# A cast on ScalarE in place of a second comparison on VectorE, while the first and third coefficient tables are built

## The chip, the cores and the metric

The kernel runs on one core of one Trainium2 chip. The metric is the device time of one execution in microseconds (us); lower is better. The engines are named as in the profile: PE (TensorE matmuls), PEld (its weight loads), DVE (VectorE), ACT (ScalarE), POOL (GpSimd) and SP (SyncE, which here only issues DMAs).

## The reference, cut to what matters

One transformer layer runs over 640 tokens of 1024 numbers: 128 context tokens and 512 latent tokens, that is five blocks of 128 tokens. The change lies in the second half of the layer, a retrieval from 16,384 single-neuron experts:

```
s1, s2 = scores of the query halves against 128 keys each, per head (8 heads)
v1, i1 = top_k(s1, 16);  v2, i2 = top_k(s2, 16)
top, sel = top_k(v1[:, None] + v2[None, :], 16)      # 16 experts a head
eidx = i1 * 128 + i2 of the chosen ones;  gate = softmax(top)
act = gelu(x . u[eidx])                               # one dot product per chosen expert
y = sum over 8 heads x 16 of gate * act * v[eidx]
```

Each token thus has 128 chosen experts (8 x 16), each with a coefficient `gate * act`, and each expert number splits into a first key `eidx >> 7` and a second key `eidx & 127`.

## The kernel before

**The u side.** For all five blocks the rows `u[eidx]` are gathered: one indirect DMA of POOL per chosen expert fetches one row of 1024 numbers for each of the 128 tokens (512 KB), and one DVE instruction (`scalar_tensor_tensor` over 1024 columns) makes the 128 dot products. There are 640 such gathers, in order of the blocks, 128 a block. The text calls the pair of them "a gather".

**The v side.** For block 4 the rows of v are gathered in the same way (128 more gathers at the very end). For blocks 0 to 3 they are not: there the sum over experts is a dense product with all of v, on PE. For it each block needs a **table** of 128 x 128 coefficients per token, most of them zero. `Dense.build(b)` makes the table of block b (b = 0, 1, 2, 3: the first to the fourth table), and `Dense.product(g)` multiplies two tables with v, which is streamed in by SP as 128 pieces of 512 KB: product 0 takes the first and second table, product 1 the third and fourth.

**One table.** The inner loop of `build` runs 64 times, over two tokens each; the text calls one turn **a pair**. For the two tokens, with the 128 chosen experts on the partitions, it makes two one-hot matrices of 128 x 128: `B_` from the second keys and `A_` from the first keys, the latter scaled by the coefficients. Two matmuls (`B_` transposed times `A_`, 128 x 128 x 128) then give the tables of the two tokens. The engines share a pair as follows: DVE compares a row of numbers 0 to 127 (`iota2`, bf16) with the keys twice, once into `eq` (bf16, 256 columns) and once into `B_` (f32, 256 columns); ACT multiplies `eq` by the coefficients into `A_` (two instructions of 128 columns); PE does the two matmuls; and after every second pair ACT copies 512 columns from PSUM into the table, strided for the first two tables and dense for the other two. `eq` and the pair `A_`, `B_` have two buffers each, used in turn. Table b = 2q' + q lies in memory `W[q]`, so the third table overwrites the first one while product 0 still reads it: rows n to n+3 of it are written once product 0 has used them.

**Order.** `Plan` records every instruction, gives each an estimated cost, and lists them by a forward and backward pass over the engines; each engine then runs its list strictly in order. A changed instruction therefore moves others too: which gathers, top-k steps and matmuls stand between the pairs is decided anew. Main work (lane 0) and gathers (lane 1) compete for DVE. All instructions are issued from one line, L365, so the profile is read by operation and tile. In it `arena` is the large SBUF tile in which tables, one-hot matrices and streamed rows lie, `iota` is `iota2`, `w` are the buffers of streamed weights and of v, `dots` the dot products.

**Stages.** The key scores of blocks 2 to 4 (`key_scores`, matmuls 128 x 384 with weights wq) run on PE while the first table is begun; then the rest of the first table and the second; then product 0, with the third table beside its second half and the beginning of the fourth at its end; then the rest of the fourth; then product 1, beside the last u gathers and all v gathers.

Of the kernel before, what the change touches and what calls it, by code (L numbers as in the profile page):

```python
# [12 lines left out]
BF16 = mybir.dt.bfloat16  # L13
# [3 lines left out]
AF = mybir.ActivationFunctionType  # L17
OP = mybir.AluOpType
# [3 lines left out]
P = 128  # L22
# [346 lines left out]
def layer(ctx: ExitStack, tc: tile.TileContext, a: dict):  # L369
    nc = Plan(tc.nc)  # L370
# [9 lines left out]
    iota2 = st.tile([P, P, 2], BF16, name="iota2")  # L380
# [32 lines left out]
    def bank():  # L413
        return ps.alloc([512], lo=banks[0], hi=banks[1])
# [11 lines left out]
    def mm(out, lhsT, rhs, start, stop):  # L426
        nc.tensor.matmul(out, lhsT=lhsT, rhs=rhs, start=start, stop=stop)
        k, m = lhsT.shape[0], int(np.prod(lhsT.shape[1:]))
        n = int(np.prod(rhs.shape[1:]))
        up = lambda v: 32 if v <= 32 else 64 if v <= 64 else 128  # L430
        clk["PE"] += 4 * n / 2400.0 * up(k) / 128 * up(m) / 128

    def tr(out, in_):
        nc.tensor.transpose(out, in_, ident)
        clk["PE"] += 0.216
# [118 lines left out]
    oneh, eqs, tabs, scb, spare = [], [], [], [], []  # L554

    def reserve():

        all_ = ar.alloc([19, P], lo=0, hi=12 * 256 // UNIT).ap
        oneh[:] = [all_[:, 4 * i:4 * i + 4].rearrange("s (z n) i -> s z n i", z=2) for i in range(2)]
        eqs[:] = [all_[:, 8 + i].bitcast(BF16).rearrange("s (i n) -> s i n", n=2) for i in range(2)]  # L560
        tabs[:] = [all_[:, 12], all_[:, 13], all_[:, 14].bitcast(BF16).rearrange("s (z n) -> s z n", z=2)]
        scb[:] = [all_[:, 15:19]]
        spare[:] = [all_[:, 0:8].rearrange("s a b -> s (a b)")]
# [388 lines left out]
    def ctx_front():  # L952
# [123 lines left out]
        ada(2, 1)  # L1076
        make_gates(0, ("g2",))
        reserve()
        done.add("ctx")

# [471 lines left out]
    class Dense:  # L1552
# [5 lines left out]
        def build(self, b):  # L1558

            g, q = divmod(b, 2)  # L1560
            if self.W[q] is None:
                self.W[q] = ar.alloc([P, P], top=True)
            Wn = self.W[q].ap
            if g == 0:
                Wn = Wn.rearrange("j i n -> j n i")
            while (b, 3) not in cready:
                yield "wait"

            bt = bank()
            tr(bt.ap[:, 0:P], cw[b].rearrange("q h k -> q (h k)"))  # L1570
            cT, ti, keys = tabs
            tii = ti.bitcast(I32)
            id_ = idx[b].rearrange("q h k -> q (h k)")
            for z, (op, s) in enumerate(((OP.arith_shift_right, 7), (OP.bitwise_and, 127))):
                nc.vector.tensor_single_scalar(tii, id_, s, op=op)
                nc.vector.tensor_scalar(ti, tii, 1.0, None, op0=OP.mult)
                tr(bt.ap[:, P * (z + 1):P * (z + 2)], ti)
            nc.scalar.copy(cT, bt.ap[:, 0:P])
            nc.scalar.copy(keys, bt.ap[:, P:3 * P].rearrange("s (z n) -> s z n", z=2))
            ps.free(bt)  # L1580
            full = None
            for m in range(P // 2):
                n0 = 2 * m
                while g == 1 and self.at < min(n0 + 4, P) and n0 % 4 == 0:
                    yield "at"
                eq, A_, B_ = eqs[m % 2], oneh[m % 2][:, 0], oneh[m % 2][:, 1]
                nc.vector.tensor_tensor(eq, iota2, keys[:, 0, None, n0:n0 + 2].to_broadcast([P, P, 2]), op=OP.is_equal)
                nc.vector.tensor_tensor(B_, iota2.rearrange("s i n -> s n i"),
                                        keys[:, 1, n0:n0 + 2, None].to_broadcast([P, 2, P]), op=OP.is_equal)
                if n0 % 4 == 0:  # L1590
                    bw = bank()
                for k in range(2):
                    nc.scalar.activation(A_[:, k], eq[:, :, k], AF.Copy, scale=cT[:, n0 + k:n0 + k + 1])
                if full is not None:
                    nc.scalar.copy(*full)
                    ps.free(last)
                    full = None
                for k in range(2):
                    z = n0 % 4 + k
                    mm(bw.ap[:, P * z:P * z + P], B_[:, k], A_[:, k], True, True)  # L1600
                if n0 % 4:
                    full, last = (Wn[:, n0 - 2:n0 + 2, :], bw.ap.rearrange("j (n i) -> j n i", n=4)), bw
                    yield
            nc.scalar.copy(*full)
            ps.free(last)
# [194 lines left out]
```

## Time and profile before

| what | value |
|---|---|
| time, median of 3 runs | 1915.19 us (1913.91 to 1916.84) |
| the profiled execution's own time | 1923.32 us |
| its span | 1921.6 us |
| DMA moved in the span | 651.92 MB, 339 GB/s in the mean |
| PE, DVE, ACT busy in the span | 94%, 77%, 28% |

The profiled execution took 8.1 us (0.4%) longer than the median of the runs. Its span covers the program on the engines; 1.7 us lie around it. Busy shares are means over stages of very different kinds, so the stages are read one by one. A busy PE is not PE at its peak, since matmuls overlap.

### The profile page before, as it was taken

The page shows a single profiled execution, that of the slowest core. Times are in us where ns is not written, and L with a number is a line of the kernel's source. Part 1 is how long each engine was busy: PE and PEld are TensorE (multiplying, and loading weights), DVE is VectorE, ACT ScalarE, POOL GpSimd, SP SyncE. Part 2 cuts the span into 40 slices and gives each one's busy share as a digit, 9 for nine tenths or more (in the row PEclk, how much of TensorE's full clock was granted, in tenths as well). Part 3 has the DMA queues.
Part 4 walks back from the last instruction along what each step waited for, and adds up shares of the span by engine and source line. Part 5 has one row for each costly group of instructions (what it writes and reads, how often), then busy time and mean ns, then how long its engine had stood idle before and what let it go on. Part 6 is the DMA issues. An engine that isn't in the chain of part 4 may idle for free.

```text
span 1921.6 us, 21158 instructions
## 1 busy us (share of the span) xinstructions
PE 1801.0 (94%) x6096; PEld 1088.0 (57%) x6096; DVE 1471.6 (77%) x3785; ACT 534.2 (28%) x1368; POOL 823.9 (43%) x779
## 2 busy tenths in 40 slices
PE   7989999989899979978999999899987999999997
PEld 2437454445866556666544444455565666666665
DVE  2246897875788899999999998777999565666666
ACT  1125320223434333788311120122565000000000
POOL 0000456660034456433646544444434444444442
PEclk9998999988989989855999999899997999999999
DMA  9896878985668899866999999999988999999998
GB/s 363 311 328 246 305 246 311 386 327 177 209 232 305 311 342 396 307 207 179 337 408 408 399 397 410 378 408 407 388 256 276 410 409 409 409 410 409 409 409 335
DMA packets 200428, 651.92 MB, mean 339 GB/s; under 512 B 22380, under 2 KB 25708, under 8 KB 200184
## 3 DMA queue, kind: packets, MB, share of 16 engines
q0 software_dynamic: 110592, 402.70, 56.1%
q1 hardware_dynamic: 89720, 247.87, 34.5%
q8 instruction: 49, 0.80, 0.2%
q14 instruction: 67, 0.55, 0.1%
HBM read 639.22 MB, written 11.27 MB: 339 GB/s over the span
## 4 chain that ended last, share of the span: by engine, by line
DMA 28%; PE 27%; DVE 15%; issue 4%; ACT 2%; POOL 0%; DVEq 0%; SPq 0%; POOLq 0%; ACTq 0%
PE psum L365 27%; DMA arena<-in_u,idx 13%; DMA arena<-in_v,idx 12%; DVE arena L365 10%; ACT arena L365 2%; DVE psum L365 1%; DVE i L365 1%; DVE oh L365 1%; DMA out_y<-w 1%; DVE vi L365 1%; DMA w<-xres 1%; POOL arena L365 0%; DVE cand L365 0%; DMA arena<-in_w_out 0%; DVE idx L365 0%
## 5 line engine op out<-in xcount | busy, mean ns | idle before, releaser
L365 PE MATMUL psum<-w,arena 128*128 128x512 f32 (+1 forms) x2580 | 1105.1, 600 | 12.2 <-DVE arena L365 6.5
L365 POOL DMA_INDIRECT arena<-in_u,idx x640 | 701.1, 1096 | 929.5 <-DVE arena L365 466.4
L365 PEld LDWEIGHTS psum<-w,arena 128*128 128x128 f32 (+1 forms) x2580 | 567.2, 228 | 458.9 <-issue 296.2
L365 PE MATMUL psum<-arena 128*128 128x128 f32 (+5 forms) x2436 | 543.0, 381 | 62.7 <-DVE arena L365 35.8
L365 PEld LDWEIGHTS psum<-arena 128*128 128x128 f32 (+2 forms) x2436 | 380.3, 219 | 265.3 <-issue 144.9
L365 DVE SCALAR_TENSOR_TENSOR arena<-arena 128x1024 f32<-128x1024 f32 (+6 forms) x451 | 488.2, 1092 | 39.7 <-DMA arena<-in_u,idx 35.4
L365 DVE SCALAR_TENSOR_TENSOR arena<-arena,psum 128x1024 f32<-128x1024 f32 x256 | 308.2, 1214 | 82.3 <-DMA arena<-in_u,idx 82.3
L365 ACT ACTIVATE arena<-arena 128x128 f32<-128x128 bf16 (+8 forms) x626 | 240.0, 432 | 270.3 <-PE psum L365 119.8
L365 ACT COPY arena<-psum 128x512 f32<-128x512 f32 (+3 forms) x360 | 203.9, 579 | 316.9 <-PE psum L365 287.6
L365 DVE SCALAR_TENSOR_TENSOR psum<-arena,cw,psum 128x1024 f32<-128x1024 f32 x127 | 163.6, 1288 | 94.7 <-DMA arena<-in_v,idx 94.5
L365 DVE TENSOR_TENSOR arena<-iota,arena 128x256 f32<-128x256 bf16 (+1 forms) x512 | 162.9, 356 | 39.8 <-PE psum L365 35.0
L365 POOL DMA_INDIRECT arena<-in_v,idx x128 | 119.9, 936 | 144.3 <-DVE psum L365 115.6
L365 PE MATMUL psum<-arena,w 128*128 128x128 f32 (+1 forms) x704 | 142.0, 362 | 1.4 <-ACT arena L365 1.4
L365 PEld LDWEIGHTS psum<-arena,w 128*128 128x128 f32 x704 | 103.0, 200 | 32.5 <-ACT arena L365 2.1
L365 PE MATMUL psum<-ident,arena 128*128 128x128 f32 x372 | 66.5, 313 | 31.6 <-DVE arena L365 28.4
L365 PEld LDWEIGHTS psum<-ident,arena 128*128 128x128 f32 x372 | 51.0, 163 | 62.6 <-DVE arena L365 36.0
L365 DVE TENSOR_TENSOR arena<-arena 128x256 f32<-128x256 f32 (+7 forms) x131 | 59.8, 497 | 6.7 <-ACT arena L365 4.3
L365 DVE TENSOR_TENSOR arena<-psum,arena 128x512 f32<-128x512 f32 (+1 forms) x40 | 27.3, 687 | 40.8 <-PE psum L365 40.2
L365 ACT ACTIVATE zz<-dots 128x64 f32<-128x64 f32 x10 | 2.6, 256 | 186.9 <-DVE arena L365 186.9
L365 DVE TENSOR_REDUCE arena<-arena 128x8 f32<-128x512 f32 (+1 forms) x17 | 12.7, 745 | 42.1 <-ACT arena L365 42.1
L365 ACT ACTIVATE vi<-i 128x32 f32<-128x32 uint32 x20 | 4.7, 235 | 137.7 <-DVE i L365 137.6
L365 DVE MAX8 vi<-arena 128x8 f32<-128x128 f32 x128 | 31.1, 280 | 14.4 <-ACT arena L365 14.4
(75 smaller groups left out, 529.9 us busy)
## 6 DMA issues: line engine op xcount, KB each, us to landing
w<-in_v SPq DMA_DIRECT2D x251, 512.0 KB, 6.8
w<-in_wq SPq DMA_DIRECT2D x44, 512.0 KB, 4.8
w<-in_w_ada SPq DMA_DIRECT2D x41, 512.0 KB, 6.1
w<-in_w_in SPq DMA_DIRECT2D x24, 512.0 KB, 7.8
w<-in_w_out SPq DMA_DIRECT2D x20, 512.0 KB, 6.1
arena<-in_u,idx POOLq DMA_INDIRECT x640, 7.5
arena<-in_w_in SPq DMA_DIRECT2D x16, 512.0 KB, 10.5
arena<-in_x SPq DMA_DIRECT2D x9, 512.0 KB, 6.4
```

The lines of the kernel that those rows point to most:

```text
L365: getattr(getattr(self.nc, eng), fn)(*args, **kw)
```

## The change

`eq` becomes twice as wide (its second half lies in memory that was reserved and not used). In `build(0)` and `build(2)` (q = 0) one comparison of 512 columns in bf16 makes both one-hot matrices at once, the first keys' in `eq[:, 0]` and the second keys' in `eq[:, 1]`, and ACT casts the latter into `B_` (256 columns, bf16 to f32). In `build(1)` and `build(3)` nothing changes but the address of `eq`.

```diff
-        eqs[:] = [all_[:, 8 + i].bitcast(BF16).rearrange("s (i n) -> s i n", n=2) for i in range(2)]
+        eqs[:] = [all_[:, 8 + 2 * i:10 + 2 * i].rearrange("s a b -> s (a b)").bitcast(BF16)
+                  .rearrange("s (z i n) -> s z i n", z=2, n=2) for i in range(2)]
...
                 eq, A_, B_ = eqs[m % 2], oneh[m % 2][:, 0], oneh[m % 2][:, 1]
-                nc.vector.tensor_tensor(eq, iota2, keys[:, 0, None, n0:n0 + 2].to_broadcast([P, P, 2]), op=OP.is_equal)
-                nc.vector.tensor_tensor(B_, iota2.rearrange("s i n -> s n i"),
-                                        keys[:, 1, n0:n0 + 2, None].to_broadcast([P, 2, P]), op=OP.is_equal)
+                if q:
+                    nc.vector.tensor_tensor(eq[:, 0], iota2, keys[:, 0, None, n0:n0 + 2].to_broadcast([P, P, 2]),
+                                            op=OP.is_equal)
+                    nc.vector.tensor_tensor(B_, iota2.rearrange("s i n -> s n i"),
+                                            keys[:, 1, n0:n0 + 2, None].to_broadcast([P, 2, P]), op=OP.is_equal)
+                else:
+                    nc.vector.tensor_tensor(eq, iota2[:, None].to_broadcast([P, 2, P, 2]),
+                                            keys[:, :, None, n0:n0 + 2].to_broadcast([P, 2, P, 2]), op=OP.is_equal)
+                    nc.scalar.copy(B_, eq[:, 1].rearrange("s i n -> s n i"))
                 if n0 % 4 == 0:
                     bw = bank()
                 for k in range(2):
-                    nc.scalar.activation(A_[:, k], eq[:, :, k], AF.Copy, scale=cT[:, n0 + k:n0 + k + 1])
+                    nc.scalar.activation(A_[:, k], eq[:, 0, :, k], AF.Copy, scale=cT[:, n0 + k:n0 + k + 1])
```

Counted over the program, DVE loses 256 comparisons of 256 columns and gains 128 of 512; ACT gains 128 casts of 256 columns; PE, POOL and the DMAs keep their numbers. What the new order does is shown at three places.

**PE, where the key scores end.** The 128x384 rows are the last matmuls of the key scores, the 128x128 rows between them those of the first table (two a pair; of the long row 12 are the last scores), the `ident` rows transposes that prepare the second table. Before:

```order
L365 MATMUL psum<-arena,w_92 128x384
L365 MATMUL psum<-arena 128x128 x2
L365 MATMUL psum<-arena,w_92 128x384 x2
L365 MATMUL psum<-arena 128x128 x2
L365 MATMUL psum<-arena,w_92 128x384 x2
L365 MATMUL psum<-arena 128x128 x70
L365 MATMUL psum<-ident,cw_73 128x128
L365 MATMUL psum<-ident,arena 128x128
```

With the change:

```order
L365 MATMUL psum<-arena,w_91 128x384 x8
L365 MATMUL psum<-arena,w_92 128x384 x6
L365 MATMUL psum<-arena 128x128 x2
L365 MATMUL psum<-arena,w_92 128x384 x2
L365 MATMUL psum<-arena 128x128 x92
L365 MATMUL psum<-ident,cw_73 128x128
L365 MATMUL psum<-ident,arena 128x128
```

Before, 24 of the first table's 64 pairs stand among the key scores on PE and 40 behind them; with the change 19 stand among them and 45 behind.

**ACT, in the part of the first table behind the key scores.** ACTIVATE 128x128 makes half of an `A_`, CAST 128x256 is the new cast, COPY 128x4x128 the strided copy of two pairs into the table. With the change:

```order
L365 CAST arena<-arena 128x256
L365 ACTIVATE arena<-arena 128x128 x2
L365 COPY arena<-psum 128x4x128
L365 ACTIVATE arena<-arena 128x128
L365 CAST arena<-arena 128x256
L365 ACTIVATE arena<-arena 128x128
L365 CAST arena<-arena 128x256
L365 ACTIVATE arena<-arena 128x128 x2
L365 COPY arena<-psum 128x4x128
```

Before, the same pairs read:

```order
L365 ACTIVATE arena<-arena 128x128 x2
L365 COPY arena<-psum 128x4x128 x2
L365 ACTIVATE arena<-arena 128x128 x4
L365 COPY arena<-psum 128x4x128
L365 ACTIVATE arena<-arena 128x128 x4
L365 COPY arena<-psum 128x4x128
```

Each pair's two ACTIVATEs are joined by one CAST; the strided copies stay.

**DVE, at the end of the fourth table.** SCALAR_TENSOR_TENSOR 128x1024 is a gather's dot product, TENSOR_TENSOR `arena<-iota` a comparison (two a pair). Before, the last rows of the table are:

```order
L365 TENSOR_TENSOR arena<-iota_65,arena 128x256 x3
L365 SCALAR_TENSOR_TENSOR arena,dots_77<-arena,psum 128x1024
L365 TENSOR_TENSOR arena<-iota_65,arena 128x256 x4
L365 SCALAR_TENSOR_TENSOR arena,dots_77<-arena,psum 128x1024
L365 TENSOR_TENSOR arena<-iota_65,arena 128x256
L365 SCALAR_TENSOR_TENSOR arena,dots_77<-arena,psum 128x1024
L365 TENSOR_TENSOR arena<-iota_65,arena 128x256 x3
L365 SCALAR_TENSOR_TENSOR arena,dots_77<-arena,psum 128x1024
L365 TENSOR_TENSOR arena<-iota_65,arena 128x256
L365 SCALAR_TENSOR_TENSOR arena,dots_77<-arena,psum 128x1024
L365 TENSOR_TENSOR arena<-iota_65,arena 128x256 x3
```

With the change:

```order
L365 TENSOR_TENSOR arena<-iota_65,arena 128x256 x2
L365 TENSOR_TENSOR w_90<-w_90 128x256
L365 SCALAR_TENSOR_TENSOR arena,dots_77<-arena,psum 128x1024
L365 TENSOR_TENSOR arena<-iota_65,arena 128x256 x4
L365 SCALAR_TENSOR_TENSOR arena,dots_77<-arena,psum 128x1024
L365 TENSOR_TENSOR arena<-iota_65,arena 128x256 x3
L365 SCALAR_TENSOR_TENSOR arena,dots_77<-arena,psum 128x1024
L365 TENSOR_TENSOR arena<-iota_65,arena 128x256 x4
L365 SCALAR_TENSOR_TENSOR arena,dots_77<-arena,psum 128x1024
L365 TENSOR_TENSOR arena<-iota_65,arena 128x256 x3
L365 SCALAR_TENSOR_TENSOR arena,dots_77<-arena,psum 128x1024
L365 TENSOR_TENSOR arena<-iota_65,arena 128x256 x4
```

Five gathers stand here among 15 comparisons before and among 20 with the change. Among the fourth table's last 32 pairs there are 19 gathers before and 14 with the change, and four more of the small instructions that finish blocks 0 and 1 (as the `w_90` row). On PE, the table matmuls behind the last mixed rows and ahead of product 1's long run (cut there only by one or two single matmuls of product 1) belong to 41 pairs before and to 37 with the change; 502 product matmuls are left at that point in both.

## Rows read from the trace of the kernel before

**Rows 1.** The chain that ended last, in order of time: start, us, what.

```profile
689.46 104.77 PE psum L365 x435
...
1217.72 198.73 PE psum L365 x694
...
1488.25 14.73 DMA arena<-in_u,idx
```

**Rows 2.** Busy time by stretch (start:end, length, engines, PE clock, DMA share, GB/s).

```profile
core 0: us, PE busy (x) PEld busy (x) DVE busy (x) ACT busy (x) POOL busy (x), PEclk, DMA share, GB/s
705.50:801.80 96.30, 94.94 (x434) 65.67 (x433) 93.86 (x268) 51.61 (x121) 58.85 (x50) 1.00 1.00 380
801.80:842.30 40.50, 30.75 (x129) 27.49 (x130) 36.11 (x115) 34.65 (x83) 13.74 (x14) 0.55 0.66 201
842.30:883.50 41.20, 35.29 (x131) 28.80 (x130) 40.45 (x124) 35.33 (x87) 15.13 (x16) 0.54 0.71 215
883.50:925.00 41.50, 34.54 (x135) 28.00 (x134) 39.56 (x101) 35.37 (x83) 16.23 (x15) 0.57 0.60 179
945.00:1209.00 264.00, 262.74 (x615) 116.22 (x614) 241.21 (x842) 34.82 (x102) 137.37 (x120) 1.00 1.02 405
1218.00:1388.00 170.00, 170.00 (x576) 90.60 (x576) 138.62 (x310) 59.13 (x167) 81.34 (x87) 0.99 1.01 395
1425.00:1479.00 54.00, 35.83 (x169) 29.96 (x167) 50.14 (x129) 35.89 (x99) 21.15 (x22) 0.74 0.79 248
1488.00:1872.00 384.00, 384.00 (x896) 264.41 (x895) 234.57 (x272) 2.42 (x8) 173.23 (x185) 1.00 1.03 409
```

**Rows 3.** DVE's timeline: start, us, what; a last bracket is idle time before.

```profile
787.47 0.69 DVE L365 TENSOR_TENSOR arena<-iota,arena 128x256 bf16<-128x256 bf16 x2
...
801.08 1.16 DVE L365 TENSOR_TENSOR arena<-iota,arena 128x256 f32<-128x256 bf16 x4
...
817.55 0.28 DVE L365 TENSOR_TENSOR arena<-iota,arena 128x256 bf16<-128x256 bf16 x1
817.75 0.08 DVE L365 MATCH_VALUE_LOAD w<-vi,w 128x8 f32 x1
...
842.01 0.41 DVE L365 TENSOR_TENSOR arena<-iota,arena 128x256 f32<-128x256 bf16 x1
...
842.87 1.21 DVE L365 SCALAR_TENSOR_TENSOR arena<-arena 128x1024 f32<-128x1024 f32 x1
...
844.00 0.42 DVE L365 TENSOR_TENSOR arena<-iota,arena 128x256 f32<-128x256 bf16 x1
844.34 0.27 DVE L365 TENSOR_TENSOR cand<-vi 128x64 f32<-128x64 f32 x1
```

**Rows 4.** Groups by engine, operation and shape: busy us, mean ns of one.

```profile
L365 ACT ACTIVATE arena<-arena 128x128 f32<-128x128 bf16 x512 | 172.3, 394 | 146.9 <-PE psum L365 114.6 <-DVE arena L365 30.0 <-DVE vi L365 0.3
...
L365 ACT ACTIVATE arena<-arena 128x512 f32<-128x512 f32 x25 | 15.4, 627 | 20.8 <-DVE arena L365 20.5
...
L365 ACT ACTIVATE zz<-dots 128x64 f32<-128x64 f32 x10 | 2.6, 256 | 186.9 <-DVE arena L365 186.9
```

**Rows 5.** ACT's timeline in the first table.

```profile
815.38 1.04 ACT L365 COPY arena<-psum 128x512 f32<-128x512 f32 x1 [0.38 <-PE psum L365]
816.21 1.27 ACT L365 ACTIVATE arena<-arena 128x128 f32<-128x128 bf16 x4
...
822.92 1.91 ACT L365 COPY arena<-psum 128x512 f32<-128x512 f32 x2
...
843.14 0.39 ACT L365 ACTIVATE arena<-arena 128x128 f32<-128x128 bf16 x1
```

**Rows 6.** PE's timeline, at the third table's preparation and at product 1's start.

```profile
1217.72 0.48 PE L365 MATMUL psum<-ident,arena 128*128 128x128 f32 x1 [7.87 <-DVE arena L365]
...
1226.39 7.03 PE L365 MATMUL psum<-w,arena 128*128 128x512 f32 x16
...
1479.16 11.14 PE L365 MATMUL psum<-w,arena 128*128 128x512 f32 x22 [0.68 <-ACT arena L365]
```

**Rows 7.** The page's first line.

```profile
span 1921.6 us, 21158 instructions
```

## The prediction

> **What bounds the kernel now.** I read the chain of waits first, then busy time by stretch, then the timelines. The chain [rows 1] runs over PE where the key scores end (689.5 to 794.2 us) and from 1217.7 on while product 0 and the third table run together; behind 1488 it runs over gathers in flight. The stretches [rows 2] tell how hard that is. In 945 to 1209 (product 0) PE is busy 262.74 of 264 us and the DMAs are full (share 1.02, 405 GB/s). In 1218 to 1388 PE is busy throughout, and in 1488 to 1872 both PE (384 of 384) and the DMAs (409 GB/s) are. There no saving on DVE or ACT can shorten anything. Three stretches have slack on both: the first table behind the key scores (801.8 to 842.3, PE clock 0.55, so about the 1.2 GHz level, DMA share 0.66), the second table (842.3 to 925, likewise), and the rest of the fourth (1425 to 1479, DMA share 0.79). In all three DVE is busiest: 36.11 of 40.5, then 40.45 of 41.2 and 39.56 of 41.5, then 50.14 of 54 us. ACT has 34.65 of 40.5 in the first. So the end moves by what these three stretches gain or lose, since all behind product 1's start is full.
>
> **Price of a pair.** On DVE what counts is the distance of starts. A bf16 comparison of 256 columns starts 0.20 us ahead of the next instruction, an f32 one 0.34 [rows 3]. If the first runs at two columns in the time the second takes for one, 256 columns cost 0.14 fast and 0.28 slow, and the fixed part is 0.06. The new comparison of 512 columns, all bf16, then takes 0.06 + 0.28 = 0.34, and a pair falls from 0.54 to 0.34: 0.20 saved, 128 times, 25.6 us of DVE. Slow it would be 0.62, that is 0.08 more than before. The operands have the same kind of pattern as those of the 256-column one, so I take 0.34.
>
> No cast from SBUF of 256 columns is in the trace. ACT takes 256 ns for 64 columns and 627 ns for 512 [rows 4]; on the line between, 256 columns take 415 ns. The starts of successive ACTIVATEs lie (1.27 - 0.394) / 3 = 0.29 apart [rows 4, 5], 0.10 less than the 394 ns one lasts, so a cast holds ACT for 0.32 us. Bounds: 0.29, as one of 128 columns, and 0.43, half of a strided copy of 512, whose starts lie 1.91 - 1.04 = 0.87 apart [rows 5]. Over 128 pairs that is 41 us of new ACT work for 25.6 of DVE.
>
> The Trainium skill, "ScalarE: Activation LUTs", Rules for kernel authors, says that simple elementwise work belongs on VectorE, which per element is up to about three times as fast in bf16; that speaks against this change. Here the instruction that leaves DVE writes f32 and holds it for 0.34 us, no less than the cast holds ACT, so the trace shows no such advantage for it. The same page's figures (186 ns + 0.833 ns a column, 93 ns overlap) make the cast 0.31 as an estimate; 42 casts (below) would then sum to 0.4 us less.
>
> **First table.** Up to pair 22 PE works off key scores, and DVE is full (93.86 of 96.3 us to 801.8). Counted in the order, DVE has made 50 gathers by pair 22 instead of 45 since the table's start. A gather holds it for 844.00 - 842.87 = 1.13 us [rows 3]. So +5.7 for gathers, -22 x 0.20 = -4.4 for comparisons, about +1 for small instructions that moved ahead: pair 22, which now leaves DVE at 787.5 [rows 3], leaves it at about 790, and ACT starts on it then. From there to pair 64 ACT has 42 x (2 x 0.29 + 0.32) = 37.8 us for pairs, 18 strided copies x 0.87 = 15.7, and some 2.5 of small work (one wide cast of the top-k, the gelu): 56 us. DVE has less: over the last 32 pairs 16 gathers x 1.13 + 32 x 0.34 + some 8 of small work = 37, as long as before; there ACT has 44. So ACT becomes the bound and pair 64 leaves it no earlier than 846, with 3 to 4 us of waiting for PE and DVE at about 849.5. Now it leaves ACT at 843.1 [rows 5]. **+6.4 us**; without any wait +3, with as much idle time as ACT has now (5.9 us in 40.5) up to +10.
>
> **Second table.** Unchanged on ACT (35.3 us a half [rows 2]) and DVE-bound. The order gives DVE 33 gathers instead of 34 and 7 small instructions instead of 22 between pairs 64 and 128, since they went ahead while ACT was the bound: -1.1 and -15 x 0.2 (they start 0.2 to 0.3 apart) = -4. **-3.5**, bounds -1 and -5.
>
> **Product 0 and third table.** PE waits 7.87 us for the third table's preparation, which DVE reaches behind its gathers [rows 6]. In both orders 132 gathers lie between pair 128 and that instruction, and the DMAs that bring them are full, so the wait moves along unchanged; 12 small instructions fewer are worth 0 to -2: I take -1. The third table's 64 casts (20 us of ACT) lie beside PE's full 170 us, where ACT is busy 59.13; the 13 us that DVE saves there lie under the same cover. Were ACT late by its whole 20 us there, product 0 would end as much later.
>
> **Fourth table.** With the change 37 pairs instead of 41 are left when PE has nothing else. PE does the other 4 x 2 matmuls of 128 columns under cover but pays for them: a 512-column one takes 7.03 / 8 = 0.88 [rows 6], so 8 x 0.22 = +1.8. DVE, 50.14 of 54 us busy, has four pairs less (4 x 0.54 = -2.2) and about four gathers less (-4.5), and one or two small instructions of 0.3 more; what of this went ahead to the stretch before must fit there, where the counts of gathers and small instructions fall too. **-5**, bounds -8 and -2.
>
> **Product 1.** 502 matmuls are left in both orders, and DVE has 211 u and v gathers to go instead of 213. PE and DMAs are both full, so neither alone shortens it: 0.
>
> **Sum.** 6.4 - 3.5 - 1 - 5 = -3.1; since the wait on ACT is the least certain term I round towards the middle and take **-2 us** against the profiled execution's span of 1921.6 us [rows 7]. That execution ran 0.4% above the median of the runs, so the 2 us are taken off the median: 1915.2 - 2 = **1913.2 us**.
>
> **Rivals.** *ACT costs more than is given back (slower).* Place: pairs 22 to 64, as above, with ACT waiting as much as now (+10), second table -2, fourth table -2, wait at the third 0: +6, so 1921. For it: `eq` and `B_` have two buffers, and all of ACT's work for a pair now stands in one line, in order with the 0.87 us copies. Against it: the gathers that now delay DVE fill just these waits. It decides once pair 64 leaves ACT later than about 854. This is the way the Trainium skill's page on ScalarE, named above, would have it.
>
> *ACT hides its casts (faster).* If ACT catches up among the key scores (51.61 of 96.3 us busy there [rows 2]), DVE's sums hold: first table +1, second -3.5, fourth -6.5: -9, so 1906. Against it: the order leaves 45 pairs behind the key scores, five more than before.
>
> *The wide comparison runs at one column a cycle.* A pair then costs DVE 0.28 more than in the sum; with 64 pairs of the first table that is +18, the third's hidden by PE: 1931. Against it are the 0.20 and 0.34 of [rows 3]. The Trainium skill, "VectorE: DVE Perf Modes", What auto-detection actually checks, gives two-input operations double rate if every tensor is 16-bit with step 1; by that rule it is fast, and the 256-column rows agree.
>
> **How the numbers follow.** About 0.2%, 3.8 us, is what a measurement can tell from no change. Chances: the forecast 0.44, ACT hidden 0.32, ACT too dear 0.19, slow comparison 0.05. The forecast's own range is 1909 to 1918 (its terms' bounds partly cancel); of its 0.44, 0.32 lie within 0.2%, 0.08 faster, 0.04 slower. Of ACT hidden 0.29 is faster, of ACT too dear 0.16 slower, the rest within. Faster 0.37, within 0.2% 0.38, slower 0.25. The range goes from 1904, just past the hidden case, to 1923, just past the dear one; it leaves out the slow comparison and the tails.
>
> **What would show it.** In the profile after: the 512-column comparison near 0.41 us a piece (0.69 if slow) and the cast near 0.41; ACT above 90% busy and DVE below it in the first table behind the key scores; pair 64 about 6 us later than now; the second table shorter by 3 to 4; PE's wait ahead of the third table near 8; product 1's long run starting 1 to 5 us earlier. The prediction is wrong if the wait ahead of the third table vanishes or grows, if ACT delays PE in product 0's second half, or if product 1 does not stay at full rate.

## The result, and the profile after

The changed kernel took 1931.57 us in the median (1924.14 to 1948.30, 10 runs), the kernel before 1920.57 us (1913.91 to 1924.97, 10 runs): ratio 1.007, 95% interval 1.0049 to 1.0091, so slower by 0.7%. The prediction was 1913.2 us with a range from 1904 to 1923: wrong. It started from 1915.19 us, the median of three runs of the kernel before, and ten runs of it gave 1920.57; 5.4 us of the miss of 18.4 lie in that start, the other 13 in the change: forecast at -2 us, measured at +11.0 between the medians. The profiled execution of the changed kernel has a span of 1935.3 us, 13.7 over [rows 7].

First the prices, as groups of instructions of the changed kernel by shape (busy us, mean ns of one, idle time before them):

```profile
L365 DVE TENSOR_TENSOR arena<-iota,arena 128x512 bf16<-128x512 bf16 x128 | 53.2, 421 | 45.5 <-ACT arena L365 45.1
L365 DVE TENSOR_TENSOR arena<-iota,arena 128x256 f32<-128x256 bf16 x128 | 52.2, 426 | 2.0 <-PE psum L365 1.8
L365 ACT CAST arena<-arena 128x256 f32<-128x256 bf16 x128 | 50.7, 396 | 28.9 <-DVE arena L365 28.3 <-PE psum L365 0.2
```

The wide comparison of 512 columns takes no longer than the old one of 256 into f32, and the cast lasts what an ACTIVATE of 128 columns did ([rows 4], 394 ns). Both are as forecast. Next, five marks of the changed kernel's timelines, taken on DVE, ACT, DVE, PE and PE: the first table's first comparison, the copies that open the second table, the second table's last comparison, the transpose that prepares the third table, and the start of product 1's long run:

```profile
725.53 0.42 DVE L365 TENSOR_TENSOR arena<-iota,arena 128x512 bf16<-128x512 bf16 x1
...
871.00 1.23 ACT L365 COPY arena<-psum 128x128 f32<-128x128 f32 x2
...
953.23 0.40 DVE L365 TENSOR_TENSOR arena<-iota,arena 128x256 f32<-128x256 bf16 x1
...
1240.23 0.47 PE L365 MATMUL psum<-ident,arena 128*128 128x128 f32 x1 [5.50 <-DVE arena L365]
...
1494.18 11.09 PE L365 MATMUL psum<-w,arena 128*128 128x512 f32 x25
```

The same marks of the kernel before; its last two are in [rows 6], at 1217.72 and 1479.16:

```profile
705.58 0.48 DVE L365 TENSOR_TENSOR arena<-iota,arena 128x256 bf16<-128x256 bf16 x2
...
843.55 1.20 ACT L365 COPY arena<-psum 128x128 f32<-128x128 f32 x2
...
928.80 0.42 DVE L365 TENSOR_TENSOR arena<-iota,arena 128x256 f32<-128x256 bf16 x1
```

The first comparison, ahead of which nothing was changed in the code, comes 19.95 us later. From there to product 1's long run the changed kernel takes 768.65 us, the kernel before 773.58: 4.9 us less. So in these two executions the whole loss lies ahead of the first table. The stretches show where (the changed kernel, in pieces of 12 us):

```profile
core 0: us, PE busy (x) PEld busy (x) DVE busy (x) ACT busy (x) POOL busy (x), PEclk, DMA share, GB/s
540.00:552.00 12.00, 11.35 (x51) 10.90 (x52) 6.77 (x16) 2.31 (x6) 3.02 (x3) 0.52 0.40 114
552.00:564.00 12.00, 12.00 (x24) 5.49 (x24) 6.96 (x20) 3.47 (x7) 1.88 (x2) 0.50 0.20 65
564.00:576.00 12.00, 10.58 (x48) 6.18 (x47) 8.63 (x21) 4.55 (x15) 4.84 (x4) 0.93 0.69 202
576.00:588.00 12.00, 12.00 (x29) 5.89 (x28) 6.39 (x19) 2.49 (x10) 1.87 (x2) 0.50 0.52 145
588.00:600.00 12.00, 12.00 (x38) 7.42 (x36) 6.27 (x19) 3.34 (x8) 2.82 (x3) 0.50 0.42 125
600.00:612.00 12.00, 12.00 (x47) 8.43 (x47) 5.46 (x19) 4.50 (x14) 2.82 (x3) 0.63 0.57 189
```

The kernel before, its fall and then 564 to 612 in one row:

```profile
540.00:552.00 12.00, 11.40 (x62) 8.63 (x62) 11.84 (x30) 5.87 (x18) 3.66 (x3) 0.78 0.49 162
552.00:564.00 12.00, 12.00 (x40) 8.62 (x40) 10.70 (x27) 4.05 (x10) 6.10 (x6) 0.50 0.75 241
564.00:612.00 48.00, 48.00 (x229) 27.99 (x228) 39.64 (x113) 20.50 (x59) 22.78 (x21) 1.00 0.80 270
```

This is the attention stage, beside the gathers of block 1. In the changed kernel PE's granted clock is at 0.50, the 1.2 GHz level, from about 540 to 564, comes back for some 10 us, and is at 0.50 again from 575 to beyond 600. The kernel before falls once as well, from about 547 to 564, but has 1.00 from there to 612: the second fall is what is new. DVE and the DMAs fall with it: DVE is busy 6 of 12 us and the DMAs move 125 to 189 GB/s, against 39.64 of 48 us and 270 GB/s.

### The profile page after: what moved, and what is told of

Same layout as the page of the kernel before. It is cut to its first block, busy times and chain, and to the rows that moved or that the text cites. A ratio compares the mean times of both kernels' runs of the same rounds, so it can differ in the third digit from the quotient of the medians.

```text
span 1935.3 us, 20984 instructions
## 1 busy us (share of the span) xinstructions
PE 1812.6 (94%) x6096; PEld 1091.6 (56%) x6096; DVE 1446.4 (75%) x3657; ACT 566.9 (29%) x1496; POOL 840.3 (43%) x779
## 4 chain that ended last, share of the span: by engine, by line
DMA 34%; PE 32%; DVE 17%; issue 11%; POOL 3%; ACT 3%; SPq 0%; DVEq 0%; POOLq 0%; ACTq 0%
PE psum L365 32%; DMA arena<-in_u,idx 18%; DMA arena<-in_v,idx 12%; DVE arena L365 11%; POOL arena L365 3%; ACT arena L365 3%; DVE psum L365 1%; DMA w<-in_w_ada 1%; DVE oh L365 1%; DVE i L365 1%; DVE vi L365 1%; DMA xres<-arena 0%; DMA arena<-in_w_ada 0%; DMA arena<-in_selc 0%; DVE idx L365 0%
## 5 line engine op out<-in xcount | busy, mean ns | idle before, releaser
L365 POOL DMA_INDIRECT arena<-in_u,idx x640 | 717.1, 1121 | 924.9 <-DVE arena L365 457.0
L365 PE MATMUL psum<-arena 128*128 128x128 f32 (+5 forms) x2436 | 550.6, 382 | 70.3 <-ACT arena L365 37.7
L365 DVE SCALAR_TENSOR_TENSOR arena<-arena 128x1024 f32<-128x1024 f32 (+5 forms) x451 | 489.5, 1094 | 47.3 <-DMA arena<-in_u,idx 42.9
L365 ACT ACTIVATE arena<-arena 128x128 f32<-128x128 bf16 (+8 forms) x626 | 250.7, 435 | 229.5 <-PE psum L365 100.6
L365 DVE TENSOR_TENSOR arena<-iota,arena 128x256 bf16<-128x256 bf16 (+2 forms) x384 | 132.7, 379 | 52.4 <-ACT arena L365 49.8
L365 ACT CAST arena<-arena 128x256 f32<-128x256 bf16 x128 | 50.7, 396 | 28.9 <-DVE arena L365 28.3
L365 ACT ACTIVATE arena<-psum,arena 128x128 f32<-128x128 f32 (+2 forms) x102 | 34.6, 430 | 25.2 <-PE psum L365 24.4
```

The source lines that it names most:

```text
L365: getattr(getattr(self.nc, eng), fn)(*args, **kw)
```

## The experiments

**Two plans in one kernel.** Both versions record the same instructions at the same places of the list, except that a pair's two comparisons are a comparison and a cast. So one kernel can make both plans, and emit either version's instructions (EMIT) in the order of either plan, with one for the part up to the first table's first comparison (FRONT) and one for what follows (REST); 0 is the kernel before, 1 the changed one.

```diff
+        lists = []
+        for which in (self.FRONT, self.REST):
+            self.cur = which
+            lists.append(self.order())
+        a, b = lists
+        head = a[:a.index(self.cut)]
+        seen = set(head)
+        want = head + [i for i in b if i not in seen]
...
-        for i in self.order():
+        for i in self.merge():
```

Theory A: the order of the front costs the time, the tables do not. Rival B: the cast is too dear. Rival C: chance. Each ratio below is to the kernel before on the same chip; a gain or loss in us that goes with a ratio is that ratio times the median of the kernel before, and can differ from the difference of the two medians.

`EMIT, FRONT, REST = 1, 0, 0`:

> The changed instructions (wide comparison, cast on ACT) in the order that the kernel before has on every engine: the wide comparison stands where the first of the two comparisons stood, the cast where the second stood. Theory A (the new order of the part ahead of the first table costs the time: PE at its lower level there for longer, 20 us lost before the first table's first comparison, and the tables themselves give 6 back): first table begins near 706 us as before, PE at 1.00 from 564 to 648, time 0 to 6 us under the kernel before. Rival B (the cast is too dear for ACT): 8 to 14 us over the kernel before, lost between the first table's pairs 22 and 64. Rival C (neither; the clock of PE in the attention stage falls by chance in any execution): time between the two kernels, runs that scatter by 20 us.

Measured 1932.75 us against 1919.23, ratio 1.0064 (1.0049 to 1.0079): B's forecast, and not A's. But the front is as before (first comparison at 706.06), so this loss is another one: the copies that open the second table come at 854.65, that is 10.6 us further behind the first comparison than in the kernel before, and nothing is given back (product 1's long run at 1488.67, 9.5 later). A cast put at the second comparison's place, with gathers spread as if DVE still had both, does cost what rival B says.

`EMIT, FRONT, REST = 0, 1, 1`:

> The instructions of the kernel before (two comparisons, no cast) in the order that the changed kernel has on every engine. Theory A: first table begins near 725 us, PE at its lower level for most of 540 to 612, time 8 to 20 us over the kernel before. Rival B: as the kernel before, within 3 us, since no cast is left. Rival C: as for the other run, scatter of 20 us without regard to the order.

1937.45 us against 1919.23, ratio 1.0087 (1.0056 to 1.0117), runs from 1920.57 to 1949.05: without any cast the loss is there in full, and no smaller than the changed kernel's 1.007. Rival B falls as the cause of the result. The profiled execution, at 1927.61 us one of the quicker, begins its first table at 710.71 and not near 725; it has no second fall, and the part on why the prediction was wrong comes back to it.

`EMIT, FRONT, REST = 1, 0, 1`, in two groups of runs:

> The changed instructions; every engine follows the order of the kernel before up to the first comparison of the first table, and from there the order of the changed kernel. Theory A: the front costs nothing (first table at 706 us), and what the tables gave back in the changed kernel (6 us between the first table's start and the end) is left as a gain: 1 to 8 us under the kernel before. Rival B: 8 to 14 us over it. Rival C: no difference to the run with the old order throughout.

> The changed instructions with the front's order of the kernel before and the changed kernel's order from the first table on (as in the run with old front and new tables). Theory A: 0 to 4 us under the kernel before and 10 to 18 under the changed kernel. Theory C: as the changed kernel, within 3 us.

1917.74 against 1919.23, ratio 0.9986 (0.9973 to 0.9998), and 1916.49 against 1919.91, ratio 0.9983 (0.9969 to 0.9998). With the old front the change is a small gain, 2.7 and 3.3 us by the ratios (1.5 and 3.4 between the medians), and this version is just faster than both kernels. Its marks (second group):

```profile
701.97 0.41 DVE L407 TENSOR_TENSOR arena<-iota,arena 128x512 bf16<-128x512 bf16 x1
...
848.93 1.20 ACT L407 COPY arena<-psum 128x128 f32<-128x128 f32 x2
...
932.21 0.41 DVE L407 TENSOR_TENSOR arena<-iota,arena 128x256 f32<-128x256 bf16 x1
...
1218.77 0.47 PE L407 MATMUL psum<-ident,arena 128*128 128x128 f32 x1 [5.61 <-DVE arena L407]
...
1472.39 12.80 PE L407 MATMUL psum<-w,arena 128*128 128x512 f32 x29
```

`EMIT, FRONT, REST = 0, 1, 0`:

> The instructions of the kernel before (no cast anywhere); every engine follows the order of the changed kernel up to the first comparison of the first table, and from there the order of the kernel before. Theory A: first table near 725 us, PE at its lower level for most of 540 to 612, and the loss stays: 12 to 22 us over the kernel before. Rival B: within 3 us of it. Rival C: no difference to the kernel before in the median of five, only a wider scatter.

1934.45 us, ratio 1.0077 (1.0053 to 1.01), first comparison at 729.84: the new front alone makes the whole loss. In these four kernels the loss of the front goes with the order, so rival C falls too as the cause of the median; what is left of it is the scatter (below).

**Four matmuls.** What in the front? In the changed kernel's PE timeline ahead of the second fall stand two waits for ACT:

```profile
570.30 1.02 PE L365 MATMUL psum<-w,arena 128*128 128x512 f32 x2
571.16 0.60 PE L365 MATMUL psum<-ident,arena 128*128 128x128 f32 x4
572.49 1.33 PE L365 MATMUL psum<-arena 128*128 128x64 f32 x10 [0.73 <-ACT arena L365]
574.43 0.89 PE L365 MATMUL psum<-ident,arena 128*128 128x128 f32 x2 [0.61 <-ACT arena L365]
...
583.06 4.82 PE L365 MATMUL psum<-arena 64*128 64x128 f32 x14
```

In the order before, four 128x512 matmuls of the out-projection stand between these small ones; the changed kernel's plan has made them earlier. The next kernel is the changed one with only these four put back (numbers are places in the recorded list: what is moved, and behind what); DVE, ACT, POOL and SP keep the changed kernel's order:

```diff
+    MOVED = ((3166, 2674), (3167, 2682), (3168, 2690), (3169, 2686))
...
+        for i, p in self.MOVED:
+            want.remove(i)
+            want.insert(want.index(p) + 1, i)
```

> The changed kernel with four matmuls of the out-projection (128x512, the first weights of its second piece) placed on PE as the kernel before has them: between the small matmuls and transposes that in the changed kernel wait 0.73 and 0.61 us for ACT at 571 to 574 us. DVE, ACT, POOL and SP keep the changed kernel's order. Theory A (those two waits let PE's granted clock fall to its 1.2 GHz level for 576 to 608, and that is most of what the new front costs): PE stays at 1.00 from 566 to 640, the first table begins at 705 to 712 instead of 725, and the time is 1916 to 1924, 8 to 15 us under the changed kernel. Rival D (the new front is slower for other reasons, and the fall of the clock only shows it): 1928 to 1935, as the changed kernel, with the first table later than 718.

This first group ran on a chip where the kernel before took 1936.54 us, so the forecast times don't fit it; the kernel took 1934.17, ratio 0.9988 (0.9969 to 1.0006), with no second fall (1.00 from 576 to 660). The changed kernel has no run on that chip, so the two were taken again side by side on another:

> The changed kernel as it is, beside the next three on one chip, since chips differ by 16 us for the kernel before. Theory A (front order): 0.4 to 1.0% over the kernel before, with PE's granted clock at 0.50 twice between 530 and 612 us. If chance of the chip alone made the first result (theory C): within 0.2% of the kernel before.

> The changed kernel with the four matmuls of the out-projection back at the places that the kernel before gives them (as in the run with four matmuls back), now beside the changed kernel. Theory A: 8 to 15 us under the changed kernel, no second fall of the clock between 575 and 612. Rival D: within 3 us of the changed kernel.

The changed kernel took 1934.10 us, ratio 1.0076 (1.0047 to 1.0105); with the four matmuls back 1919.82, ratio 0.9996 (0.9982 to 1.0011). The places of four matmuls are worth 14.3 us. The old front as a whole (1916.49 in this group) is worth 17.6, so some 3 us lie elsewhere in the new front. The changed kernel's profiled execution again has the second fall (0.50 from 588 to 612) and its first comparison at 734.19. With the four matmuls back the first comparison comes at 708.28, though the first fall is as in the changed kernel (0.56 in 540 to 552, 0.50 in 552 to 564). The PE timeline reads:

```profile
569.65 1.02 PE L412 MATMUL psum<-w,arena 128*128 128x512 f32 x2
570.54 1.33 PE L412 MATMUL psum<-arena 128*128 128x64 f32 x10
571.71 1.08 PE L412 MATMUL psum<-w,arena 128*128 128x512 f32 x2
572.62 0.27 PE L412 MATMUL psum<-ident,arena 128*128 128x128 f32 x1
572.73 1.02 PE L412 MATMUL psum<-w,arena 128*128 128x512 f32 x2
...
578.80 2.60 PE L412 MATMUL psum<-arena 64*128 64x128 f32 x14
```

The two waits are gone (one of 0.36 us for ACT, at 566.63, is new), and the group of 14 that took 4.82 us at the lower level takes 2.60. DVE's waits in 564 to 612 (us in total, times, longest), in the changed kernel:

```profile
DVE arena L365 <- PE psum L365: 21.2, 11, 3.7
```

And in this one:

```profile
DVE arena L412 <- PE psum L412: 7.1, 11, 1.5
```

And the stretch 564 to 612, the changed kernel first:

```profile
564.00:612.00 48.00, 46.58 (x156) 27.92 (x155) 26.76 (x76) 14.88 (x45) 12.35 (x12) 0.64 0.55 165
564.00:612.00 48.00, 47.64 (x227) 28.08 (x225) 40.80 (x118) 21.66 (x65) 23.76 (x21) 0.99 0.79 260
```

Counted on DVE, 13 gathers are made in this stretch in the changed kernel and 20 in this one, and 206 ahead of the first comparison in both: seven gathers are made later, in front of the first table. So the way from the order to the time, as the rows have it, is: PE at 1.2 GHz for some 30 us, DVE waiting for PE, gathers late, first table late. The two waits of PE stand at its beginning; that they are what brings the clock down is argued, since moving the four matmuls also puts large matmuls back between the small ones.

The reverse, on the kernel before:

```diff
+    MOVED = ((3166, 3163), (3167, 3166), (3168, 3167), (3169, 2648))
```

> The kernel before with the same four matmuls of the out-projection moved ahead on PE, to where the changed kernel has them; nothing else is touched. Theory A: PE waits for ACT near 571, its granted clock falls to 0.50 there in part or all of the runs, the first table begins 10 to 20 us later, and the time is 8 to 15 us over the kernel before, with a wide scatter of the runs. Rival D: within 3 us of the kernel before.

1943.77 us against 1936.54, ratio 1.0026 (1.001 to 1.0042). The direction is A's, the size, 5 us by the ratio (7.2 between the medians), is less than forecast: PE waits for ACT (0.45, 0.61 and 0.44 us at 585 to 588), but the clock falls for part of 588 to 600 only (0.60 there, 0.98 in 600 to 612). The first comparison comes at 723.24; the run with the cast in the third table alone (below), which has the front of the kernel before on the same chip, has it at 717.79.

**One cast alone.** `CAST` names the tables with the cast, `CUT` the table up to which the order is that of before:

```diff
-                    if q or which == 0:
+                    if b not in nc.CAST or which == 0:
...
+    CAST, CUT = (2,), 2
```

> The kernel before with the wide comparison and the cast in the third table alone; the order is that of the kernel before up to the third table's first comparison, and planned anew from there. Theory A, with the prediction's terms: the first two tables as before, the third's casts hidden beside PE, the fourth table shorter by 2 to 8 us, product 1 begins 2 to 8 us earlier; time 1 to 6 us under the kernel before. Rival B (a cast costs ACT more than is given back, there too): 0 to 5 us over it.

> The cast in the third table alone, in the order of the kernel before up to there (as in the run with the cast in the third only). Theory A with the prediction's terms: 1 to 6 us under the kernel before, and 0 to 4 under the run with the old front and both casts. If both casts together are the better version, it lies over that run instead.

1932.79 against 1936.54, ratio 0.9983 (0.9966 to 0.9999), and 1918.45 against 1919.91, ratio 0.9988 (0.9971 to 1.0005): 3.3 and 2.3 us under by the ratios, the second not told from nothing. It was also forecast to lie under the old front with both casts (1916.49 in that group); it lies 2 us over, and no difference can be told. And with `CAST, CUT = (0,), 0`:

> The kernel before with the wide comparison and the cast in the first table alone; the order is that of the kernel before up to the first table's first comparison, and planned anew from there. Theory A, with the prediction's terms: pair 64 some 6 to 9 us later, 1 to 5 of it given back in the second table; product 1 begins 2 to 7 us later and the time is 2 to 7 us over the kernel before. Rival E (the part behind the first table takes up what is lost there, or more): within 2 us of the kernel before or under it.

1946.06 against 1936.54, ratio 1.0043 (1.0024 to 1.0061), 8.3 us over by the ratio (9.5 between the medians), a little more than forecast. The cast in the first table alone is a loss.

## Why the prediction was wrong

The step that failed is the sentence under **What bounds the kernel now**: "So the end moves by what these three stretches gain or lose". It set the loss ahead of the first table at zero without a term. It wasn't zero: the plan is made over the whole program, its backward passes carry the tables' costs to the front, and there the new order moved four matmuls past small ones that wait for ACT. Their 14.3 us are more than four times the net sum, and the whole front's 17.6 more than five times. The working counted gathers "since the table's start", as if that start stood still; the range left this out as well, and no rival had it.

The terms themselves can be read from the marks, as differences of each distance to the kernel before (us):

| stretch | forecast | changed kernel | old front, first and second group |
|---|---|---|---|
| start to the first comparison | none | +19.9 | +1.2, -3.6 |
| first table, to the copies that open the second | +6.4 | +7.5 | +7.7, +9.0 |
| second table | -3.5 | -3.0 | -2.3, -2.0 |
| from there to the third's preparation | -1 | -1.9 | -1.7, -2.4 |
| third and fourth table, to product 1's long run | -5 | -7.5 | -5.1, -7.8 |
| sum over the tables | -3.1 | -4.9 | -1.5, -3.2 |

- **Prices.** Right: 421 ns for the wide comparison, 396 for the cast (0.41 each forecast). The rival of a slow comparison falls.
- **First table.** The sum is near (7.5 to 9.0 us for 6.4), but its two halves are not, and that they cancel is luck. The first two rows cut the changed kernel's first table where ACT begins pair 22, the next two the kernel before at the same places; the last is the beginning of the changed kernel's second table:

```profile
725.53:814.43 88.90, 86.63 (x366) 57.19 (x365) 83.49 (x241) 46.23 (x118) 68.22 (x51) 1.00 1.01 388
814.43:870.83 56.40, 42.81 (x197) 35.55 (x195) 50.94 (x144) 56.16 (x156) 22.56 (x23) 0.70 0.77 263
...
705.58:787.66 82.08, 82.08 (x355) 55.32 (x355) 80.37 (x232) 37.99 (x89) 54.84 (x46) 1.00 1.02 392
787.66:843.53 55.87, 44.76 (x214) 38.97 (x212) 50.75 (x156) 49.51 (x120) 17.75 (x18) 0.67 0.72 230
...
871.00:910.00 39.00, 29.20 (x120) 24.93 (x120) 35.25 (x90) 36.60 (x82) 12.66 (x13) 0.60 0.58 173
```

Up to pair 22 about 2.5 us were forecast, and it is 6.8 (6.4 and 8.4 with the old front). The working added up DVE, with a gather at 1.13 us. But the DMAs are full there in both kernels (1.02 and 1.01), so the five more gathers that the order puts ahead of pair 22 would cost their transfer, about 6.8 us as an estimate (5 x 512 KB at 388 GB/s), whatever the comparisons save. DVE now waits there for gathers to land, in all 5.2 us, eight times, which it does not do in the kernel before:

```profile
DVE arena L365 <- DMA arena<-in_u,idx: 5.2, 8, 1.0
```

PE's order leads to the same place: its last key scores end 88 us after the first comparison in both kernels, now with 19 pairs made among them instead of 24. Which of the two holds pair 22 was not separated. From there to the end of pair 64, 4 us more were forecast, and it is 0.5 (1.1 and 0.4 with the old front). ACT does become the bound, as forecast, with DVE below it: busy 56.16 of 56.40 us, where it had 49.51 of 55.87. But the casts go into the idle time that ACT had. In the second table ACT is still busier than DVE at first (36.60 of 39.00 us against 35.25), which was not forecast.

- **Wait ahead of the third table.** It went from 7.87 [rows 6] to 5.50 us, not on unchanged, and so the term is -1.9 instead of -1.
- **Fourth table.** Right in size. Its mechanism is less sure: with the cast in the first table alone the stretch from the third's preparation on is shorter too (by 7.1 us in its profile), with the cast in the third alone by 3.7 and 0.3 us in the two profiles. So at least part of the gain probably comes from gathers made while the first table was held up; no run shows which.
- **Sum.** A gain of 2 us was forecast; with the old front, 2.7 and 3.3 us were measured. In one profile these terms scatter by 1 to 3 us, so the sum is better held by the medians. With the new front held (the run without the cast at 1.0077, the changed kernel at 1.007 and 1.0076) no gain of the tables can be told.

That the loss follows the fall of the clock, and not the order as such, can be read from four profiles. The changed kernel (twice), the two comparisons in its order, and the new front with the old tables have, as far as the traces record it, the same instructions in the same order on DVE, ACT, POOL and PE up to the first comparison. All four have the same two waits of PE. In three the granted clock drops within a microsecond of the second wait's end, and the first comparison comes at 725.53, 734.19 and 729.84. In the fourth, that of the two comparisons, it does not drop:

```profile
571.64 1.33 PE L407 MATMUL psum<-arena 128*128 128x64 f32 x10 [0.73 <-ACT arena L407]
573.58 0.74 PE L407 MATMUL psum<-ident,arena 128*128 128x128 f32 x2 [0.61 <-ACT arena L407]
```

Its stretch 564 to 612, and that of the new front with the old tables, which fell:

```profile
564.00:612.00 48.00, 46.55 (x226) 27.68 (x224) 39.87 (x115) 21.74 (x66) 22.81 (x20) 1.00 0.78 263
564.00:612.00 48.00, 46.55 (x158) 28.17 (x156) 26.42 (x76) 14.20 (x44) 13.11 (x13) 0.64 0.53 160
```

The execution that did not fall took 1927.61 us and began its first table at 710.71, 15 to 23 us ahead of the three; others of the same kernel took up to 1949.05. So the waits alone do not bring the fall every time, and what decides stays open. With the four matmuls in their old places the second fall is in neither of two profiles.

## What to carry to other kernels

Where a planner sets the order, a changed cost moves instructions everywhere: compare the orders ahead of the change as closely as behind it, engine by engine, and look above all at what now stands between small matmuls that wait for another engine. To judge a change apart from the plan that it gets, run both versions' instructions in both orders. Here a saving on an engine paid only where the order was planned for it: in the old order the same cast cost 0.6%, with the tables planned anew and the front kept it gained 0.15%. And where the DMAs are full, count a gather that moves ahead by its transfer as well as by the instruction that uses it; here the two gave 6.8 and 5.7 us for five gathers, and 6.8 was measured, with nothing to be seen of what the comparisons saved.

## What the runs showed of the hardware that was not expected

The scatter of the changed kernel goes with PE's mean granted clock. Of nine runs on one chip the four at 0.929 to 0.931 took 1941.87 to 1946.98 us, three at 0.933 to 0.938 took 1931.88 to 1934.10, and two at 0.940 and 0.942 took 1923.94 and 1924.01. The kernel with the four matmuls back stayed within 1915.78 to 1925.73 at 0.940 to 0.948. Between kernels the mean says less: the profiled execution of the kernel before took 1923.32 us, that of the changed one 1937.11, both at 0.935.

One program can differ by more between two chips than by the change. The kernel with the cast in the third table alone took 1918.45 us on one and 1932.79 on the other. Its two profiled executions have spans 12.2 us apart, and the first comparison comes 13.7 us later in the longer one (704.11 and 717.79). On the slower chip PE waits for ACT at 531, a wait that the faster one's timeline doesn't have, and PE's clock is at 0.58 in 528 to 540 and at 0.50 from 540 to 576 (1.00, 0.81 and 0.50 up to 564 on the other):

```profile
531.11 2.38 PE L412 MATMUL psum<-arena 128*128 128x128 f32 x8 [3.21 <-ACT arena L412]
```

ACT itself stands idle there ahead of a copy, and the profile names no engine of the core that released it:

```profile
530.79 0.27 ACT L412 COPY arena<-psum 128x128 f32<-128x128 f32 x1 [4.57 <-remote]
```

All four profiles from this chip have such a wait of ACT, ending between 527 and 533 (2.0 us in one, 4.6 in three), and none of the ten others has one there. So again some 3 us of waiting on PE go with some 14 us at the end. What ACT waited for is not in the traces, and whether it belongs to the chip or to that group of runs was not tested.
